# The 64-row products of a two-block kernel alternate between two PSUM banks and the two row halves, and the second feed-forward takes its spare weight buffers later

## The chip, the cores and the metric

The kernel runs on one core of one Trainium2 chip. The metric is device microseconds of one execution, the median of three runs. The engines are named as the profile names them: PE (TensorE, the matrix engine), DVE (VectorE), ACT (ScalarE), POOL (GpSimd) and SP (SyncE, which issues the loads).

## The reference, cut to what matters

256 rows of 1024 numbers pass through a two-layer block and then a hybrid block, all in fp32. The parts that the change touches:

```python
# layer 1: gated linear attention, 4 heads, chunks of 64 rows
state = state * dec[..., None] + jnp.einsum('bhtk,bhtv->bhkv', ke, vv)
...
# layer 2: chunk attention, 16 heads of 64
s = jnp.einsum('bhtd,bhjd->bhtj', qi, kb).astype(jnp.float32) + bias
p = jax.nn.softmax(jnp.where(mb, s, NEG_INF), axis=-1).astype(vb.dtype)
return jnp.einsum('bhtj,bhjd->bhtd', p, vb)
...
# after each of the two layers: y = squared_relu_mlp(u, w1, w2), then a layer norm
...
# hybrid block: 8 index heads of 64 choose the 64 best keys, 8 heads of 64 attend to them
s = jnp.einsum('bqhd,bkd->bhqk', iqb, ik).astype(jnp.float32) * (IDX_DIM ** -0.5)
score = jnp.einsum('bqh,bhqk->bqk', w, jax.nn.relu(s))
_, idx = lax.top_k(score, k_top)
sc = jnp.einsum('bqhd,bqkhd->bhqk', qb, kg).astype(jnp.float32) * (Dh ** -0.5)
p = jax.nn.softmax(sc, axis=-1)
```

The contraction of the state update is over 64 rows of a chunk, that of the scores and index scores over the 64 numbers of a head. These are the 64-row products of the title. Every other matrix product contracts over 128 partitions at a time.

## The kernel before, in words

The 256 rows are two halves of 128, h = 0 and h = 1. The program passes through six phases: gated linear attention, feed-forward, chunk attention, second feed-forward, hybrid mixer, convolutional feed-forward. In each, weights arrive in chunks of 128x1024 fp32 that SP loads into one of four buffers `raw`. ACT rounds a chunk to a high part (`hi`, line 257) and DVE takes the difference as a low part (`lo`, line 262); a product is then three matmuls, `mm3` (lines 266 to 268). There are eight pairs of `hi` and `lo`. A few chunks, named by a table (`_spare`, lines 172 to 180), take another pair instead, `qk0`/`v0` or `qk1`/`v1`: the buffers in which the attentions keep keys and values. In the second feed-forward these are its second chunk and every fifth after it.

The kernel's PSUM tiles are banks of 128x512 fp32: two for tag `pc`, two for `ps` (projections), four for `y`. The score loop `core_scores` (lines 742 to 765) takes one `y` bank at a time. A bank holds 512 score columns: four heads of 128 keys for h = 0, two heads of 256 keys for h = 1. `banks` orders the heads so that one bank holds only even heads, whose queries and keys lie in partitions 0 to 63, and the next only odd heads, in partitions 64 to 127. The bank's matmuls (line 754) are followed by an addition on DVE (line 817 in chunk attention, 934 in the hybrid mixer), the maximum on DVE (758), one exponential a head on ACT (760), and, after the next bank's scores have been written down, four transposes on PE (373, operands `const` and `cs`) and a copy on ACT (769). The products with the values (line 780) come later. The loop is a generator: each `next` is called between chunks of the value projection, so that matmuls of that projection stand between the banks.

The chunk attention does its heads in two groups of eight, g = 0 and 1, each for both halves. The index scores (line 908) fill two banks (h = 0) or four (h = 1), one after another. The states of gated linear attention (line 727) use partitions 0 to 63 for the first chunk of a half and 64 to 127 for the second.

The order on each engine is not written by hand: a list scheduler orders the instructions from their dependences, estimated costs and priorities, and `prefetch` decides when a weight load may be issued. So an edit in one place moves instructions around it on every engine. Between scores DVE also works through products of the conditioning vector with its weights (line 300), one 128x1024 pass for each loaded block.

Of the kernel before, what the change touches and what calls it, by code (L numbers as in the profile page):

```python
# [172 lines left out]
def _spare():  # L173

    out = {}
    for a, b, pairs in ((ENDS[0] - 1, ENDS[1] + 1, (0, 1)), (ENDS[2] - 4, ENDS[2] - 3, (0,)),
                        (ENDS[2] + 1, ENDS[3] + 1, (0, 1)), (ENDS[4] - 8, ENDS[5], (0, 1))):
        for n, i in enumerate(range(a, b, SP)):
            out[i] = pairs[n % len(pairs)]
    return out  # L180
# [5 lines left out]
class K:  # L186
# [450 lines left out]
    def gla_core(self, h, lr, q, k, v, box):  # L637
# [57 lines left out]
        S2 = self.states(h, 0, er, v, dec)  # L695
# [9 lines left out]
        if h == 0:  # L705
            self.S = S2
            self.S = self.states(h, 1, er, v, dec)
# [10 lines left out]
    def states(self, h, c, er, v, dec):  # L718

        nc = self.nc  # L720
        out = []
        r = slice(c * 64, c * 64 + 64)
        for j in range(2):
            p = self.pc()
            for d2 in range(2):
                d = j * 2 + d2
                nc.tensor.matmul(p[:, d2 * 256:d2 * 256 + 256], er[r, d * 128:d * 128 + 128], v[r, d * 256:d * 256 + 256], start=True, stop=True)
            S = self.sb(512, "bias", 4)
            if self.S is None:
                nc.scalar.activation(S, p, AF.Copy)  # L730
            else:
                for d2 in range(2):
                    hs = slice(d2 * 256, d2 * 256 + 256)
                    nc.vector.scalar_tensor_tensor(S[:, hs], self.S[j][:, hs], dec[:, j * 2 + d2, c:c + 1], p[:, hs], op0=ALU.mult, op1=ALU.add)
            out.append(S)
        return out
# [5 lines left out]
    def core_scores(self, h, qT, kT, pts, sums, score):  # L742
# [5 lines left out]
        last = None  # L748

        for n, hs in enumerate(self.banks(nb)):  # L750
            p = self.bank()
            for i, hd in enumerate(hs):
                r0 = (hd % 2) * 64
                nc.tensor.matmul(p[:, i * N:i * N + N], qT[r0:r0 + 64, hd // 2, :], kT[r0:r0 + 64, hd // 2, :N], start=True, stop=True)  # L754
            s = score(hs[0], nb, p)
            sv = s.rearrange("p (a n) -> p a n", n=N)
            mx = self.sb(4, "mx", 4)
            nc.vector.tensor_reduce(mx[:, :nb], sv, axis=AX.X, op=ALU.max, negate=True)
            for i in range(nb):
                nc.scalar.activation(sv[:, i, :], sv[:, i, :], AF.Exp, bias=mx[:, i:i + 1], accum_out=sums[:, hs[i]:hs[i] + 1])  # L760
            if last is not None:
                self.core_turn(last, pts[n - 1])
            last = s
            yield
        self.core_turn(last, pts[n])
# [105 lines left out]
    def hyb_phase(self, h, after):  # L871
# [32 lines left out]
        for hs in self.banks(nb):  # L904
            p = self.bank()
            for i, hd in enumerate(hs):
                r0 = (hd % 2) * 64
                nc.tensor.matmul(p[:, i * N:i * N + N], iqT[r0:r0 + 64, hd // 2, :], self.ikT[r0:r0 + 64, :N], start=True, stop=True)
            rl = self.cs()[:, :512]
            nc.scalar.activation(rl, p, AF.Relu, scale=0.125)  # L910
            for i, hd in enumerate(hs):
                if hd == 0:
                    nc.vector.tensor_scalar(sc, rl[:, 0:N], iw[:, 0:1], None, op0=ALU.mult)
                else:
                    nc.vector.scalar_tensor_tensor(sc, rl[:, i * N:i * N + N], iw[:, hd:hd + 1], sc, op0=ALU.mult, op1=ALU.add)
# [21 lines left out]
        qT = None  # L937
# [455 lines left out]
```

## Time and profile before

| | |
|---|---|
| three runs | 1060.17, 1054.99, 1059.1 us; median 1059.1 us |
| the profiled execution | 1057.73 us, of which its span is 1055.9 us |
| busy share of the span | PE 96%, DVE 72%, ACT 54%, POOL 3% |
| mean granted TensorE clock | 0.995 |
| DMA | 228.98 MB, mean 217 GB/s |

The span runs from the first to the last recorded instruction; 1.8 us of the execution lie outside it. "Busy" on PE counts a matmul from its start to a modelled end, and matmuls overlap in that count, so the pitch from one start to the next is what a matmul costs. The trace shows each fp32 matmul of the 64-row products as two instructions. An engine's row in a timeline begins with its start and its length in us, and ends in brackets with the idle time before it and the instruction that ended that idle time.

### The profile page before, as it was taken

The numbers are of one execution on the slowest core, as the hardware profiler recorded it, in microseconds if no ns is written. First come the engines' busy times: TensorE is split into PE (matmuls) and PEld (weight loads), VectorE is DVE, ScalarE is ACT, GpSimd is POOL, SyncE is SP. The second block draws the span as 40 slices with busy tenths as digits, with TensorE's granted clock in tenths as the row PEclk, the third lists the DMA queues.
The fourth block names the chain that finished last, engine by engine and source line by source line (L and its number), as shares of the span: only waits on it lengthen the run. The fifth ranks groups of instructions, "written<-read, shape, count | busy, mean of one in ns | idle before, by whom it ended". The sixth has DMA issues, their size and how long they took to land.

```text
span 1055.9 us, 15168 instructions
## 1 busy us (share of the span) xinstructions
PE 1017.6 (96%) x5628; PEld 850.0 (80%) x5628; DVE 763.3 (72%) x1186; ACT 567.6 (54%) x869; POOL 33.8 (3%) x77
## 2 busy tenths in 40 slices
PE   6999999999998999999999999999999999999997
PEld 4777777898986758677889988777878788999996
DVE  6878898777677886749656644898445678877764
ACT  4664466545455454536655553576454378555543
POOL 0000200000000000000000000000000001000000
PEclk9999999999999999999999999999999999999999
DMA  9888868888885787825877654344346455655521
GB/s 341 331 298 301 309 201 282 306 304 298 284 297 179 218 295 247 286 92 184 287 229 249 227 166 145 120 145 149 106 164 213 162 179 182 217 185 192 183 80 40
DMA packets 69478, 228.98 MB, mean 217 GB/s; under 512 B 7430, under 2 KB 12806, under 8 KB 69404
## 3 DMA queue, kind: packets, MB, share of 16 engines
q1 hardware_dynamic: 69404, 228.01, 64.2%
q8 instruction: 44, 0.72, 0.3%
q14 instruction: 30, 0.25, 0.1%
HBM read 226.93 MB, written 1.05 MB: 216 GB/s over the span
## 4 chain that ended last, share of the span: by engine, by line
PE 63%; DVE 9%; DMA 7%; ACT 3%; issue 3%; POOL 1%; POOLq 0%; DVEq 0%; ACTq 0%; SPq 0%
PE ps L268 12%; PE ps L266 12%; PE ps L267 12%; PE y L266 8%; PE y L268 8%; PE y L267 7%; DMA raw<-in_w_dram 6%; DVE lo L262 2%; PE y L780 1%; PE pc L373 1%; ACT hi L257 1%; DMA raw<-in_ada_dram 1%; PE y L373 1%; PE y L754 1%; DVE x L393 1%
## 5 line engine op out<-in xcount | busy, mean ns | idle before, releaser
L262 DVE TENSOR_TENSOR lo<-raw,hi 128x1024 fp32r<-128x1024 f32 (+3 forms) x290 | 306.5, 1068 | 132.8 <-ACT hi L257 129.4
L257 ACT ACTIVATE hi<-raw 128x1024 fp32r<-128x1024 f32 (+2 forms) x250 | 262.4, 1054 | 252.1 <-PE y L268 66.9
L266 PE MATMUL ps<-hi,uh 128*128 128x512 f32 (+3 forms) x408 | 160.4, 394 | 2.3 <-ACT uh L365 0.9
L267 PE MATMUL ps<-lo,uh 128*128 128x512 f32 (+3 forms) x408 | 158.2, 388 | 1.2 <-DVE lo L1260 1.1
L266 PE MATMUL y<-hi,hh 128*128 128x512 f32 x378 | 152.9, 404 | 5.3 <-ACT hh L274 5.2
L268 PE MATMUL ps<-hi,ul 128*128 128x512 f32 (+3 forms) x408 | 157.5, 386 | 0.2 <-DVE ul L366 0.2
L267 PE MATMUL ps<-ul,hi 128*128 128x256 f32 x536 | 151.4, 282 | 0.0
L268 PE MATMUL ps<-uh,lo 128*128 128x256 f32 x536 | 151.1, 282 | 0.0
L266 PE MATMUL ps<-uh,hi 128*128 128x256 f32 x536 | 151.0, 282 | 0.0
L268 PE MATMUL y<-hi,hl 128*128 128x512 f32 x378 | 149.8, 398 | 0.4 <-DVE hl L275 0.4
L267 PE MATMUL y<-lo,hh 128*128 128x512 f32 x378 | 150.2, 397 | 0.0
L266 PEld LDWEIGHTS ps<-uh,hi 128*128 128x128 f32 x536 | 100.9, 188 | 2.3
L267 PEld LDWEIGHTS ps<-ul,hi 128*128 128x128 f32 x536 | 100.6, 188 | 2.3
L268 PEld LDWEIGHTS ps<-uh,lo 128*128 128x128 f32 x536 | 101.3, 189 | 0.0
L266 PEld LDWEIGHTS ps<-hi,uh 128*128 128x128 f32 x408 | 77.5, 190 | 19.3 <-ACT uh L365 1.5
L267 PEld LDWEIGHTS ps<-lo,uh 128*128 128x128 f32 x408 | 77.5, 190 | 16.8 <-DVE lo L1260 3.0
L268 PEld LDWEIGHTS ps<-hi,ul 128*128 128x128 f32 x408 | 77.4, 190 | 15.8 <-issue 0.9
L266 PEld LDWEIGHTS y<-hi,hh 128*128 128x128 f32 x378 | 71.5, 189 | 21.4 <-ACT hh L274 6.6
L268 PEld LDWEIGHTS y<-hi,hl 128*128 128x128 f32 x378 | 71.3, 189 | 18.2 <-DVE hl L275 1.2
L267 PEld LDWEIGHTS y<-lo,hh 128*128 128x128 f32 x378 | 71.4, 189 | 14.8 <-issue 0.7
L262 DVE TENSOR_TENSOR v<-raw,qk 128x1024 fp32r<-128x1024 f32 (+1 forms) x49 | 52.0, 1069 | 26.7 <-ACT qk L257 26.1
L257 ACT ACTIVATE qk<-raw 128x1024 fp32r<-128x1024 f32 x42 | 44.5, 1060 | 49.7 <-DMA raw<-in_w_dram 28.7
(290 smaller groups left out, 1500.0 us busy)
## 6 DMA issues: line engine op xcount, KB each, us to landing
raw<-in_w_dram SPq DMA_DIRECT2D x302, 512.0 KB, 4.3
raw<-in_ada_dram SPq DMA_DIRECT2D x80, 512.0 KB, 4.6
br<-in_rows_dram SPq DMA_DIRECT2D x12, 256.0 KB, 5.4
bias<-in_relb_dram SPq DMA_DIRECT2D x12, 256.0 KB, 6.2
lng<-in_rows_dram SPq DMA_DIRECT2D x5, 512.0 KB, 4.8
raw<-in_w_dram SPq DMA_DIRECT2D x8, 256.0 KB, 6.7
lnb<-in_rows_dram SPq DMA_DIRECT2D x4, 512.0 KB, 6.1
z<-in_ada_dram SPq DMA_DIRECT2D x3, 512.0 KB, 7.4
```

What stands on the lines that cost most here:

```text
L257: self.nc.scalar.activation(hi, raw, AF.Copy)
L262: self.nc.vector.tensor_sub(lo[:, sl], raw[:, sl], hi[:, sl].bitcast(F32))
L266: mm(out, xh, wh, start=start, stop=False)
L267: mm(out, xh, wl, start=False, stop=False)
L268: mm(out, xl, wh, start=False, stop=stop)
L373: self.nc.tensor.transpose(p[:, k * 128:k * 128 + 128], src[:, k * 128:k * 128 + 128], self.ident)
L393: nc.vector.tensor_mul(x[:, sl], x[:, sl], self.lng[:, sl])
L754: nc.tensor.matmul(p[:, i * N:i * N + N], qT[r0:r0 + 64, hd // 2, :], kT[r0:r0 + 64, hd // 2, :N], start=True, stop=True)
L780: nc.tensor.matmul(o[:, hd * 64:hd * 64 + 64], pT[:, (i * nkb + kb) * 128:(i * nkb + kb) * 128 + 128], v[:, kb, hd * 64:hd * 64 + 64], sta ...
```

## The change

Three places are rewritten and one number is moved. `states` makes the products of both chunks of a half together where both are wanted (h = 0), with one `pc` bank for each chunk, and alternates between the chunks. `core_scores` takes two `y` banks at a time, one of even and one of odd heads, and alternates between them matmul by matmul; only then come the additions, maxima and exponentials of both banks, and after them the transposes of the two banks before. It yields twice for each two banks. The index scores alternate in the same way. In `_spare` the first chunk of the second feed-forward that takes a spare pair is its sixth where it was its second.

```diff
-                        (ENDS[2] + 1, ENDS[3] + 1, (0, 1)), (ENDS[4] - 8, ENDS[5], (0, 1))):
+                        (ENDS[2] + 5, ENDS[3] + 1, (0, 1)), (ENDS[4] - 8, ENDS[5], (0, 1))):
...
-        S2 = self.states(h, 0, er, v, dec)
+        S2, *S3 = self.states(er, v, dec, 2 - h)
...
+            ps = [self.pc() for _ in range(n)]
             for d2 in range(2):
                 d = j * 2 + d2
-                nc.tensor.matmul(p[:, d2 * 256:d2 * 256 + 256], er[r, d * 128:d * 128 + 128], v[r, d * 256:d * 256 + 256], start=True, stop=True)
...
+                for c, p in enumerate(ps):
+                    r = slice(c * 64, c * 64 + 64)
+                    nc.tensor.matmul(p[:, d2 * 256:d2 * 256 + 256], er[r, d * 128:d * 128 + 128], v[r, d * 256:d * 256 + 256], start=True, stop=True)
...
-        for n, hs in enumerate(self.banks(nb)):
-            p = self.bank()
-            for i, hd in enumerate(hs):
-                r0 = (hd % 2) * 64
-                nc.tensor.matmul(p[:, i * N:i * N + N], qT[r0:r0 + 64, hd // 2, :], kT[r0:r0 + 64, hd // 2, :N], start=True, stop=True)
...
+        for n in range(0, len(groups), 2):
+            two = groups[n:n + 2]
+            ps = [self.bank() for _ in two]
+            for hs in zip(*two):
+                for p, hd in zip(ps, hs):
+                    i = two[hd % 2].index(hd)
+                    r0 = (hd % 2) * 64
+                    nc.tensor.matmul(p[:, i * N:i * N + N], qT[r0:r0 + 64, hd // 2, :], kT[r0:r0 + 64, hd // 2, :N], start=True, stop=True)
+            new = []
+            for hs, p in zip(two, ps):
+                s = score(hs[0], nb, p)
...
+                new.append(s)
+            for m, s in enumerate(last):
+                self.core_turn(s, pts[n - 2 + m])
+            last = new
             yield
-        self.core_turn(last, pts[n])
+            yield
+        for m, s in enumerate(last):
+            self.core_turn(s, pts[n + m])
```

The work is the same, and so is the number of matmuls of each kind but for the spare chunks (12 in the second feed-forward, before 13). The 64-row products stood in 26 unbroken runs on PE and stand in 19. In the changed file the scores are at line 761, the maximum at 767, the copy at 781 and the index scores at 922.

First, PE in the first head group of the chunk attention, where h = 0's second score bank and h = 1's first were apart. Before, from h = 0's first bank (`y_3478`; `y_3506` is h = 1's first, `y_3530` h = 0's second):

```order
L754 MATMUL y_3478<-qk_668_3243,ep_677_3285 128x128 x2
L266 MATMUL ps_3499<-hi_3256,uh_72 128x512
L267 MATMUL ps_3499<-lo_3257,uh_72 128x512
L268 MATMUL ps_3499<-hi_3256,ul_73 128x512
L266 MATMUL ps_3499<-hi_3256,uh_72 128x512
L267 MATMUL ps_3499<-lo_3257,uh_72 128x512
L268 MATMUL ps_3499<-hi_3256,ul_73 128x512
L754 MATMUL y_3506<-qk_668_3243,ep_692_3368 128x256 x2
```

After, the same place (`y_3478` and `y_3479` are h = 0's two banks), from the second of two pieces into which its scores are split:

```order
L761 MATMUL y_3478<-qk_668_3243,ep_677_3285 128x128
L761 MATMUL y_3479<-qk_668_3243,ep_677_3285 128x128
L761 MATMUL y_3478<-qk_668_3243,ep_677_3285 128x128
L761 MATMUL y_3479<-qk_668_3243,ep_677_3285 128x128
L761 MATMUL y_3478<-qk_668_3243,ep_677_3285 128x128
L761 MATMUL y_3479<-qk_668_3243,ep_677_3285 128x128
L266 MATMUL ps_3515<-hi_3256,uh_72 128x512
L267 MATMUL ps_3515<-lo_3257,uh_72 128x512
L268 MATMUL ps_3515<-hi_3256,ul_73 128x512
```

Both banks of h = 0 now stand together and alternate. Behind them come three more `mm3`-matmuls, h = 1's two banks, and then 18 matmuls of the projection before the first transposes of `cs`.

Second, PE in the second head group, at the first transposes. Before, the transposes of h = 0's first bank (`cs_3948`) stand seven rows behind h = 1's first scores:

```order
L754 MATMUL y_3968<-qk_777_3673,ep_805_3805 128x256 x2
L266 MATMUL ps_3933<-hi_3731,uh_72 128x512
L267 MATMUL ps_3933<-lo_3732,uh_72 128x512
L268 MATMUL ps_3933<-hi_3731,ul_73 128x512
L266 MATMUL ps_3933<-hi_3731,uh_72 128x512
L267 MATMUL ps_3933<-lo_3732,uh_72 128x512
L268 MATMUL ps_3933<-hi_3731,ul_73 128x512
L754 MATMUL y_3992<-qk_777_3673,ep_802_3786 128x128 x4
L373 MATMUL y_4008<-const_70,cs_3948 128x128 x4
```

After, the last rows of the 18 projection matmuls that follow h = 1's scores, and the transposes of both of h = 0's banks (`cs_3953`, `cs_3964`):

```order
L266 MATMUL ps_3933<-hi_3769,uh_72 128x512
L267 MATMUL ps_3933<-lo_3770,uh_72 128x512
L268 MATMUL ps_3933<-hi_3769,ul_73 128x512
L373 MATMUL y_4042<-const_70,cs_3953 128x128 x4
L373 MATMUL y_4048<-const_70,cs_3964 128x128 x4
L266 MATMUL ps_3977<-hi_3769,uh_72 128x512
L267 MATMUL ps_3977<-lo_3770,uh_72 128x512
```

Eight transposes now stand together, behind three times as many projection matmuls.

Third, DVE at the start of the second feed-forward. Before, the low part of its second chunk (`v_922`, of the spare pair) stands behind the residual and the statistics of h = 1 (`x_10`):

```order
L405 SCALAR_TENSOR_TENSOR x_10_75<-x_10_75,z_4394 128x512
L366 TENSOR_TENSOR ul_73<-t_911_4261,uh_72 128x512
L406 BN_STATS st_4395<-x_10_75 128x6
L262 TENSOR_TENSOR v_922_4337<-raw_4334,qk_921_4336 128x512
L408 BN_AGGR mv_4402<-st_4395 128x2
L262 TENSOR_TENSOR v_922_4337<-raw_4334,qk_921_4336 128x512
```

After, the second, third and fourth chunk (`lo_4288`, `lo_4305`, `lo_4322`, all of the eight ordinary pairs) stand among the norm of h = 0 (`x_9`), ahead of h = 1's residual:

```order
L262 TENSOR_TENSOR lo_4288<-raw_4285,hi_4287 128x512
L410 TENSOR_SCALAR rv_4238<-mv_4236 128x1
L262 TENSOR_TENSOR lo_4288<-raw_4285,hi_4287 128x512
L412 TENSOR_SCALAR rv_4238<-mv_4236,rv_4238 128x1
L275 TENSOR_TENSOR hl_928_4346<-y_4340,hh_927_4345 128x512
L414 TENSOR_SCALAR x_9_74<-x_9_74,rv_4238 128x512
L262 TENSOR_TENSOR lo_4305<-raw_4302,hi_4304 128x512 x2
L262 TENSOR_TENSOR lo_4322<-raw_4319,hi_4321 128x512
L393 TENSOR_TENSOR x_9_74<-x_9_74,lng_3233 128x512
L262 TENSOR_TENSOR lo_4322<-raw_4319,hi_4321 128x512
```

The second chunk's low part moved up some 20 rows on DVE, and the third's and fourth's with it.

## Rows read from the trace of the kernel before

**Rows 1.** The page, busy time: engine, us, share of the span, instructions.
```profile
PE 1017.6 (96%) x5628; PEld 850.0 (80%) x5628; DVE 763.3 (72%) x1186; ACT 567.6 (54%) x869; POOL 33.8 (3%) x77
```
**Rows 2.** What PE waited for: us in total, times, longest us.
```profile
PE y L373 <- ACT cs L760: 2.9, 4, 1.3
PE ps L267 <- DVE v L262: 2.3, 1, 2.3
```
**Rows 3.** PE's timeline at a states run: start us, length us.
```profile
97.31 1.99 PE L727 MATMUL pc<-v,hl 64*128 64x256 f32 x8 [1.01 <-DVE z L693]
99.23 0.70 PE L704 MATMUL y<-bias,cs 128*128 128x256 f32 x2
```
**Rows 4.** PE's timeline around two score runs of the first head group.
```profile
375.20 0.40 PE L268 MATMUL ps<-hi,ul 128*128 128x512 f32 x1
375.53 1.13 PE L754 MATMUL y<-qk,ep 64*128 64x256 f32 x4
376.58 0.50 PE L266 MATMUL ps<-hi,uh 128*128 128x512 f32 x1
376.92 0.40 PE L267 MATMUL ps<-lo,uh 128*128 128x512 f32 x1
377.15 0.40 PE L268 MATMUL ps<-hi,ul 128*128 128x512 f32 x1
...
378.18 1.16 PE L754 MATMUL y<-qk,ep 64*128 64x128 f32 x8
379.27 0.51 PE L266 MATMUL ps<-hi,uh 128*128 128x512 f32 x1
```
**Rows 5.** PE's timeline at the index scores and one hybrid score run.
```profile
690.90 1.71 PE L908 MATMUL y<-ikT,t 64*128 64x128 f32 x16
692.54 0.42 PE L266 MATMUL ps<-hi,uh 128*128 128x328 f32 x1
...
701.76 2.10 PE L908 MATMUL y<-ikT,t 64*128 64x256 f32 x16
703.79 0.50 PE L268 MATMUL ps<-hi,ul 128*128 128x512 f32 x1
...
727.32 1.17 PE L754 MATMUL y<-qk,ep 64*128 64x256 f32 x12
728.66 0.33 PE L373 MATMUL y<-const,cs 128*128 128x128 f32 x1 [0.17 <-ACT cs L760]
```
**Rows 6.** PE's timeline, three transposes that waited.
```profile
390.28 0.33 PE L373 MATMUL y<-const,cs 128*128 128x128 f32 x1 [1.31 <-ACT cs L760]
...
441.29 0.33 PE L373 MATMUL y<-const,cs 128*128 128x128 f32 x1 [1.07 <-ACT cs L760]
...
712.92 0.66 PE L373 MATMUL pc<-const,t 128*128 128x128 f32 x4 [1.83 <-DVE t L869]
```
**Rows 7.** DVE's timeline in the first head group.
```profile
378.79 1.22 DVE L300 SCALAR_TENSOR_TENSOR raw<-raw,crow 128x1024 f32<-128x1024 f32 x1
...
383.10 0.68 DVE L758 TENSOR_REDUCE mx<-cs 128x2 f32<-128x512 f32 x1
```
**Rows 8.** ACT's timeline, the first and last exponential of one bank of four heads.
```profile
378.91 0.40 ACT L760 ACTIVATE cs<-cs,mx 128x128 f32<-128x128 f32 x1 [3.52 <-DVE mx L758]
...
380.37 0.19 ACT L760 ACTIVATION_READ_ACCUMULATOR cs<-cs,mx 128x1 f32 x1
```
**Rows 9.** PE's timeline at the start of the second feed-forward.
```profile
482.45 0.39 PE L266 MATMUL ps<-hi,uh 128*128 128x512 f32 x1
485.16 0.50 PE L267 MATMUL ps<-v,uh 128*128 128x512 f32 x1 [2.31 <-DVE v L262]
```
**Rows 10.** Stretches: us, busy time of each engine, PEclk, DMA share, GB/s.
```profile
486.00:489.30 3.30, 3.30 (x10) 2.47 (x10) 2.86 (x7) 0.81 (x1) 0.84 (x1) 0.53 0.64 210
713.00:720.00 7.00, 7.00 (x34) 5.62 (x35) 7.00 (x19) 3.97 (x5) 0.00 (x0) 1.00 0.39 130
```
**Rows 11.** DVE's timeline in the hybrid mixer, a step of the top-k search.
```profile
712.86 0.40 DVE L921 MATCH_REPLACE8 gnorm<-m,gnorm 128x256 f32<-128x256 f32 x1
```

More of the change, by code (lines that the diff above doesn't have):

```diff
@@ L705, in gla_core @@
         if h == 0:
-            self.S = S2
-            self.S = self.states(h, 1, er, v, dec)
+            self.S = S3[0]
         yield
@@ L716, in gla_core, with states @@
         box["r"] = r
-    def states(self, h, c, er, v, dec):
+    def states(self, er, v, dec, n):
         nc = self.nc
-        out = []
-        r = slice(c * 64, c * 64 + 64)
+        out = [[], []]
         for j in range(2):
-            p = self.pc()
+            ps = [self.pc() for _ in range(n)]
             for d2 in range(2):
                 d = j * 2 + d2
-                nc.tensor.matmul(p[:, d2 * 256:d2 * 256 + 256], er[r, d * 128:d * 128 + 128], v[r, d * 256:d * 256 + 256], start=True, stop=True)
[L728 to L736, printed above, removed]
+                for c, p in enumerate(ps):
+                    r = slice(c * 64, c * 64 + 64)
+                    nc.tensor.matmul(p[:, d2 * 256:d2 * 256 + 256], er[r, d * 128:d * 128 + 128], v[r, d * 256:d * 256 + 256], start=True, stop=True)
+            for c, p in enumerate(ps):
+                S = self.sb(512, "bias", 4)
+                before = out[0][j] if c else self.S and self.S[j]
+                if before is None:
+                    nc.scalar.activation(S, p, AF.Copy)
+                else:
+                    for d2 in range(2):
+                        hs = slice(d2 * 256, d2 * 256 + 256)
+                        nc.vector.scalar_tensor_tensor(S[:, hs], before[:, hs], dec[:, j * 2 + d2, c:c + 1], p[:, hs], op0=ALU.mult, op1=ALU.add)
+                out[c].append(S)
+        return out[:n]
     @staticmethod
@@ L747, in core_scores @@
         nb = 512 // N
-        last = None
-        for n, hs in enumerate(self.banks(nb)):
-            p = self.bank()
-            for i, hd in enumerate(hs):
-                r0 = (hd % 2) * 64
-                nc.tensor.matmul(p[:, i * N:i * N + N], qT[r0:r0 + 64, hd // 2, :], kT[r0:r0 + 64, hd // 2, :N], start=True, stop=True)
[L755 to L763, printed above, removed]
+        groups = self.banks(nb)
+        last = []
+        for n in range(0, len(groups), 2):
[9 more added lines that the diff above has]
+                s = score(hs[0], nb, p)
+                sv = s.rearrange("p (a n) -> p a n", n=N)
+                mx = self.sb(4, "mx", 4)
+                nc.vector.tensor_reduce(mx[:, :nb], sv, axis=AX.X, op=ALU.max, negate=True)
+                for i in range(nb):
+                    nc.scalar.activation(sv[:, i, :], sv[:, i, :], AF.Exp, bias=mx[:, i:i + 1], accum_out=sums[:, hs[i]:hs[i] + 1])
+                new.append(s)
+            for m, s in enumerate(last):
+                self.core_turn(s, pts[n - 2 + m])
+            last = new
             yield
-        self.core_turn(last, pts[n])
+            yield
+        for m, s in enumerate(last):
+            self.core_turn(s, pts[n + m])
     def core_turn(self, s, pT):
@@ L903, in hyb_phase @@
         sc = self.scam[:, h * 256:h * 256 + N]
[L904 to L915, printed above, removed]
+        groups = self.banks(nb)
+        for two in (groups[n:n + 2] for n in range(0, len(groups), 2)):
+            ps = [self.bank() for _ in two]
+            for i, hs in enumerate(zip(*two)):
+                for p, hd in zip(ps, hs):
+                    r0 = (hd % 2) * 64
+                    nc.tensor.matmul(p[:, i * N:i * N + N], iqT[r0:r0 + 64, hd // 2, :], self.ikT[r0:r0 + 64, :N], start=True, stop=True)
+            for hs, p in zip(two, ps):
+                rl = self.cs()[:, :512]
+                nc.scalar.activation(rl, p, AF.Relu, scale=0.125)
+                for i, hd in enumerate(hs):
+                    if hd == 0:
+                        nc.vector.tensor_scalar(sc, rl[:, 0:N], iw[:, 0:1], None, op0=ALU.mult)
+                    else:
+                        nc.vector.scalar_tensor_tensor(sc, rl[:, i * N:i * N + N], iw[:, hd:hd + 1], sc, op0=ALU.mult, op1=ALU.add)
         nc.gpsimd.affine_select(sc, sc, pattern=[[-1, N]], base=h * 128, channel_multiplier=1, compare_op=ALU.is_ge, fill=NEG)
```

## The prediction

> **What bounds the kernel now.** I read the page first, then PE's waits, then PE's timeline in the stages that the change touches. On the page PE is busy for 96% of the span and no other engine comes near [rows 1]; the reader is to see that time is won where PE issues less or waits less, and hardly elsewhere. PE's waits are few. Those of the touched stages are four for exponentials (2.9 us), one for a low part of a weight chunk (2.3 us) [rows 2], and one for the rotation of a query or key (1.8 us) [rows 6]. The rest of the touched stages is PE issuing matmuls back to back, so I price those from start to start.
>
> **Price of a 64-row run.** Eight 256-column instructions of the states take 99.23 - 97.31 = 1.92 us [rows 3], four of the scores 376.58 - 375.53 = 1.05 us [rows 4]. The difference gives 0.217 us for one and 0.18 us fixed. Eight of 128 columns take 379.27 - 378.18 = 1.09 us [rows 4], less 0.18 that is 0.114 each. At the run's edges the pitch of the neighbours grows from 0.23 to 0.33 and 0.34 us [rows 4], 0.21 more. An unbroken run thus costs 0.39 us beside its instructions.
>
> **Price of two row halves at once.** The kernel before shows this already, by accident of order, where banks of opposite halves stand next to each other. Sixteen 256-column index instructions would take 16 x 0.217 + 0.18 = 3.65 us one by one; they took 2.03 [rows 5], so 1.62 of a possible 1.74 was hidden (93%). They change halves every four instructions. The run of four 256-column and eight 128-column instructions would take 1.96; it took 1.34 - 0.17 = 1.17 [rows 5], 0.79 of 0.87 hidden. The index run that changes halves only once, after eight instructions, took 1.64 instead of 2.00 [rows 5]: 0.36 of 0.91. So halves overlap when they are in different banks and within a few instructions of each other. The new order alternates every matmul, that is every two instructions, which no row shows. I take the 93%; the bounds are 40%, from the run that changes once, and 100%.
>
> The Trainium skill, page "TensorEngine Tiling (Array Packing)", section "Key Properties", says that different tiles of the array can load weights and multiply in parallel, with no reserve. By that rule all would be hidden, and the sum below would be 0.6 us larger; the rows show 93% at best [rows 5], and I go by them.
>
> **The change part by part.** Runs are counted in the order of the engine, before and after.
> - Chunk attention, first head group: 10 runs become 6, 4 x 0.39 = 1.56 us. Hidden: eight 128-column instructions (0.91), four 256-column (0.87), and of the last four only two (0.43), because transposes stand between the others; 2.21 x 0.93 = 2.05. Together 3.6.
> - Second group: 6 runs become 3, 1.17. Hidden 0.91 + 0.87 + 0.87 = 2.65, x 0.93 = 2.46. Together 3.6.
> - Hybrid scores: 5 runs become 4, 0.39. Hidden 0.68 + 0.87 + 0.87 = 2.42 (one pair is cut by transposes), x 0.93 = 2.25, less the 0.79 that was hidden before. Together 1.85.
> - Index scores: h = 0 gets 0.91 x 0.93 - 0.36 = 0.5; h = 1 overlapped already, 0.
> - States: 3 runs become 4, -0.39; two chunks now stand side by side and could hide 0.87. But two `pc` banks are all there are, and the third bank waits for a copy of the first. I take 0, with -0.4 and +0.5 as bounds.
>
> PE's issue falls by 9.55 us. Against it stand the waits, since the second bank of a pair now ends its softmax behind the first. An addition and a maximum take about 0.6 us each (their length of 0.68 less its overlap) [rows 7], a bank's exponentials 380.37 + 0.19 - 378.91 = 1.65 [rows 8].
> - First group: DVE alternates these steps with conditioning passes of 1.2 us [rows 7], and the order puts the second bank's maximum into the place of the one at 383.10. It ends at 383.7, and the first transpose of that bank can start near 384.3, a head after. PE's rows up to there (6 matmuls, a pair run, 18 matmuls, four transposes, 5 matmuls) end near 383.0: a wait of 1.3 us. For the next pair I find another 0.7. The old wait of 1.31 [rows 6] goes. Net -0.7, bounds 0 and -2.3.
> - Second group: from the end of h = 0's scores to the transposes PE has 6 + 18 matmuls at 0.234 and a pair run, 6.9 us. The second bank needs 0.6 x 3 for addition, addition and first maximum, then 2 x 1.65 on ACT, 5.1 us. It is covered by 1.8 us, and the old wait of 1.07 [rows 6] disappears: +1.1. If that cover were gone the price is the same 1.3 as in the first group.
> - Hybrid mixer: the rotation that PE waited for (1.83 us) [rows 6] comes two search steps later, about 0.4 us each [rows 11], but four more matmuls (0.94 us) stand ahead of its transpose: 0. The next rotation but one stands behind one more 128x1024 pass (1.2 us, as the conditioning pass) [rows 7]: -1.0. Behind h = 1's first scores PE has only 3 + 9 matmuls and a few edges, 4.0 us, where the second bank needs 5.1: -1.1; after the last pair -0.6. Net -2.7, bounds 0 and -4.5.
>
> The same page's section "Performance Considerations", under "PSUM Bottleneck", speaks against the change: tiling makes TensorE faster, not the emptying of PSUM, which can become the limit. The lengths of the steps that empty the banks bear it out so far [rows 7, 8]; the first rival below is this mechanism, and by the rule the result would be its 1054.7 us.
>
> **The spare chunks.** PE stood for 2.31 us before the low part of the second chunk [rows 9], because DVE made it behind the residual and statistics of h = 1. Behind that wait PE's granted clock was 0.53 for 3.30 us [rows 10], 0.47 x 3.30 = 1.55 us of work lost; the wait of 1.83 us that ended at 712.92 left the clock at 1.00 [rows 6, 10]. In the new order the low parts of chunks two to four stand on DVE ahead of h = 1's residual, the second's some 20 rows earlier. The wait and its half clock, 3.9 us, should go. DVE then does about one half-pass more (0.6 us) before the inputs of h = 0, whose readers have some slack; I take off 0.6. Net +3.2, bounds 0 (the wait only moves to another chunk or to h = 1's norm) and +3.9. What is late next is h = 1's norm, with 22 matmuls of cover behind its place.
>
> **Sum.** 9.55 - 0.7 + 1.1 - 2.7 + 3.2 = 10.4 us off. The profiled execution took 1057.7 us, 1.8 of it outside the span, and would take 1047.3; against the median of the three runs, 1059.1, it is 1048.7. I say 1048.5. The three runs themselves lie 0.5% apart, and about 0.5% (5.3 us) is what this measurement can tell from no change.
>
> **The rivals.**
> - *The softmax eats it.* The second bank's exponentials wait behind the first's, and the projection's matmuls don't cover them. I counted 3.7 us of such waits at three places; if each of the six score pairs costs its full 1.65 us [rows 8], that is 9.9, 6.2 more: 1054.7 us. For: DVE and ACT already end PE's waits here [rows 2]. Against: 18 matmuls stand behind two of the pairs. Chance 0.17.
> - *The halves don't overlap in the new pattern.* Every change of half costs like a run's edge, so that alternating each matmul hides nothing. Then only the fewer runs remain, 3.1 us, and the 2.8 us hidden before are lost; with the waits and the spare chunks as above the gain is 0.3 - 0.7 + 1.1 - 2.7 + 3.2 = 1.2: 1057.9. Against it speak three rows [rows 5]. Chance 0.08.
> - *The ordinary pairs run short.* Chunks two to five of the second feed-forward all need one of the eight ordinary pairs while the attention's output weights still hold some, loads are held back, and the 3.2 us turn into a loss of the same size: 1054.9. For: the chunk in the spare pair needed none of the eight. Against: it was just this chunk that came late. Chance 0.07.
> - *Slower.* A pair takes two of the four `y` banks and its transposes two more, so a late copy holds up both. If PE stands at a pair for 0.6 + 0.6 + 1.65 = 2.85 us, that is longer than the 2.31 after which the clock fell, and the half clock adds 1.55: 4.4 us a place. Without the counted waits the gain is 14.1, so it is used up at three to four of the six places and the kernel is slower by over 0.5% from five; at all six, 1071. Against: it needs the same long wait where 6.9 us of matmuls stand over a need of 5.1. Chance 0.06.
>
> My forecast has the remaining 0.62. Without any new wait, with the whole 3.9 and the states at +0.5 it reaches 1044; with only 40% hidden (8.2 x 0.53 = 4.3 less) and no gain from the spare chunks, 1056. The range is 1043.5 to 1057, which holds most of the first and third rival too. Faster by over 0.5% means below 1053.8: all but a little of the forecast and a part of two rivals, 0.68; within 0.5% 0.26; slower 0.06.
>
> **What would show it.** Right: pair runs of four 256-column matmuls (eight instructions) in about 1.1 us instead of 1.9, of eight 128-column matmuls (16 instructions) in about 1.1 instead of 2.0; no wait for a low part and a clock of 1.00 at the start of the second feed-forward; PE's sum of waits for exponentials near 4 us. Wrong: runs that take the serial time (no overlap); waits of 1.5 us and more before transposes in every group (softmax); waits for `raw`, `hi` or `lo` in the second feed-forward (pairs short); stretches with a clock near 0.5 in the attention (slower).

## The result: 0.5% faster, a little over half of what was forecast

| | before | after |
|---|---|---|
| median, 20 runs each on one chip | 1057.96 us | 1052.11 us |
| range of the runs | 1052.91 to 1064.66 | 1047.91 to 1059.25 |
| profiled execution, span | 1057.73, 1055.9 us | 1050.37, 1048.6 us |
| mean granted clock | 0.995 | 0.991 |

The ratio is 0.995, with a 95% interval from 0.9931 to 0.997: 5.9 us between the medians, where the forecast was 10.6 (1048.5 against 1059.1). The interval leaves no doubt of the sign; it doesn't tell 4 us from 7.

The pairs of banks run as they were meant to. PE's timeline after, at a pair run of the first head group and at the first run of index scores:

```profile
373.68 1.13 PE L761 MATMUL y<-qk,ep 64*128 64x256 f32 x8
374.74 0.50 PE L266 MATMUL ps<-hi,uh 128*128 128x512 f32 x1
...
684.04 1.16 PE L922 MATMUL y<-ikT,t 64*128 64x128 f32 x16
685.13 0.42 PE L266 MATMUL ps<-hi,uh 128*128 128x328 f32 x1
```

Eight 256-column instructions take 374.74 - 373.68 = 1.06 us. Four took 1.05 before [rows 4] and eight of the states 1.92 [rows 3]. Sixteen of 128 columns take 1.09 us, as eight did [rows 4]. In these runs the second half of the work costs nothing. The start of the second feed-forward is also as forecast: PE no longer waits for a low part of a weight chunk there [rows 9].

What PE waited for after (us in total, times, longest), the rows that answer to [rows 2] and the new ones:

```profile
PE pc L373 <- DVE t L851: 2.5, 2, 1.8
...
PE pc L373 <- DVE t L881: 2.4, 3, 1.9
PE y L792 <- DVE v L846: 1.8, 1, 1.8
PE y L373 <- ACT cs L769: 1.6, 2, 0.8
```

The wait for the low part (`v L262`, 2.3 us) is gone and those for exponentials look smaller. A new one has come: the value products (line 792) wait 1.8 us for DVE's addition to the values (line 846). PE's timeline in the second head group shows more than the list does:

```profile
432.33 3.02 PE L373 MATMUL y<-const,cs 128*128 128x128 f32 x8 [0.79 <-ACT cs L769]
435.11 0.48 PE L266 MATMUL ps<-hi,uh 128*128 128x512 f32 x1
...
437.76 1.09 PE L373 MATMUL y<-const,cs 128*128 128x128 f32 x8
438.60 0.48 PE L266 MATMUL ps<-hi,uh 128*128 128x512 f32 x1
...
443.21 1.79 PE L792 MATMUL y<-v,gnorm 128*128 128x64 f32 x8 [1.78 <-DVE v L846]
444.76 0.77 PE L266 MATMUL ps<-hi,hh 128*128 128x512 f32 x1
445.33 0.63 PE L267 MATMUL ps<-lo,hh 128*128 128x512 f32 x1
```

The first eight transposes take 2.78 us, the next eight 0.84: between the first ones PE waits head by head, another 1.9 us inside one row. And behind the 1.78 us the matmuls of 512 columns last 0.63 instead of 0.39 us. The stretches from there on (length, busy time by engine, PEclk, DMA share, GB/s):

```profile
443.20:446.50 3.30, 3.29 (x14) 3.00 (x14) 2.30 (x4) 0.93 (x4) 0.00 (x0) 0.53 0.76 206
446.50:449.00 2.50, 2.50 (x10) 2.31 (x11) 0.98 (x2) 0.00 (x0) 0.00 (x0) 0.50 0.85 324
449.00:453.00 4.00, 4.00 (x18) 2.93 (x18) 2.41 (x7) 1.66 (x2) 0.00 (x0) 0.84 0.51 147
```

The clock is at the lower of its two levels, 1.2 instead of 2.4 GHz, for some 7 us: 0.47 x 3.3 + 0.50 x 2.5 + 0.16 x 4 = 3.4 us of work lost. In the first group the waits for the key transposes (1.81 at 368.75) and for exponentials are about as long as before.

Where the time went is read best by counting. The products of weights (lines 266 to 268) are 4824 in both traces, in nearly one order, so the start of the n-th tells how far ahead a kernel is. The table gives the gain over the profiled execution of before between such marks, for every kernel below too: the first head group (before: 361.4 to 427.0 us), the second (to 457.5), the start of the second feed-forward (478.0 to 513.6), and the hybrid mixer (660.1 to 769.8).

| kernel | group 1 | group 2 | 2nd FF start | hybrid | whole | ratio to before, 95% interval |
|---|---|---|---|---|---|---|
| changed | +2.2 | -2.0 | +3.2 | +1.2 | +7.4 | 0.995 (0.9931 to 0.997) |
| spare_only | -1.2 | +0.7 | +2.7 | +1.0 | -0.1 | 0.9971 (0.9945 to 0.9997) |
| no_spare | +2.8 | -1.8 | +0.5 | +0.7 | +2.3 | 0.9998 (0.9973 to 1.0023) |
| one_half | +2.8 | +2.1 | +3.1 | 0.0 | +8.6 | 0.9942 (0.9915 to 0.9968) |
| bank_by_bank | -3.4 | +0.8 | +2.8 | +2.1 | +1.9 | 0.9935 (0.9907 to 0.9963) |
| spread | -1.5 | +2.5 | +2.7 | +1.6 | +3.3 | 0.998 (0.9955 to 1.0004) |
| hi_first | +3.2 | +0.3 | +2.8 | +0.4 | +8.4 | 0.9946 (0.9918 to 0.9973) |
| g1_single | -1.2 | -0.2 | +2.9 | +1.2 | +2.5 | 0.9957 (0.9928 to 0.9985) |
| bias_no_load | +0.9 | +1.9 | +2.7 | +1.5 | +2.8 | 0.9963 (0.9932 to 0.9994) |
| att_one_half | +2.3 | +1.2 | +2.9 | +1.2 | +10.2 | 0.9933 (0.9911 to 0.9955) |
| att_single | +2.0 | +0.7 | +2.6 | +1.5 | +5.7 | 0.9972 (0.9953 to 0.9991) |
| ada_no_load | +6.6 | +4.4 | +2.2 | +1.5 | +21.8 | 0.9807 (0.9782 to 0.9832) |
| warm | +0.7 | +0.2 | +2.5 | +1.6 | +4.2 | 0.9969 (0.9952 to 0.9986) |

A row is one execution. Waits and the clock behind them differ from one execution to the next: spare_only has the attention of before, and its first group came out 1.2 us longer. Before the attention too, a wait at the end of the first feed-forward, which the change doesn't touch, and the half clock beside it cost up to 3.7 us more than in before. The column of the second feed-forward hardly moves among the kernels with the new spare table; those of the attention are to be read as a tendency. The ratio is made from 4 runs of a kernel (ada_no_load) to 20, against runs of before on the same chip. The profiled executions of spare_only and bank_by_bank were the slowest of theirs, 5.8 and 7.5 us above their medians.

### The profile page after: what moved, and what is told of

It is laid out like the page before. It is cut to its first block, busy times and chain, and to the rows that moved or that the text cites. A ratio compares the mean times of both kernels' runs of the same rounds, so it can differ in the third digit from the quotient of the medians.

```text
span 1048.6 us, 15164 instructions
## 1 busy us (share of the span) xinstructions
PE 1011.4 (96%) x5628; PEld 845.8 (81%) x5628; DVE 760.1 (72%) x1186; ACT 567.0 (54%) x869; POOL 35.4 (3%) x77
## 3 DMA queue, kind: packets, MB, share of 16 engines
HBM read 226.93 MB, written 1.05 MB: 217 GB/s over the span
## 4 chain that ended last, share of the span: by engine, by line
PE 50%; DMA 13%; DVE 11%; issue 6%; ACT 5%; POOL 1%; POOLq 0%; ACTq 0%; SPq 0%; DVEq 0%
DMA raw<-in_w_dram 12%; PE ps L266 9%; PE ps L268 9%; PE ps L267 9%; PE y L266 6%; PE y L268 6%; PE y L267 6%; DVE lo L262 4%; ACT hi L257 3%; PE y L792 2%; PE pc L373 1%; DVE raw L300 1%; DMA bias<-in_relb_dram 1%; PE y L373 1%; ACT cs L769 1%
## 5 line engine op out<-in xcount | busy, mean ns | idle before, releaser
L262 DVE TENSOR_TENSOR lo<-raw,hi 128x1024 fp32r<-128x1024 f32 (+3 forms) x293 | 307.5, 1062 | 128.4 <-ACT hi L257 122.5
L262 DVE TENSOR_TENSOR v<-raw,qk 128x1024 fp32r<-128x1024 f32 (+1 forms) x46 | 50.7, 1106 | 27.3 <-ACT qk L257 27.0
```

What stands on the lines that cost most here:

```text
L262: self.nc.vector.tensor_sub(lo[:, sl], raw[:, sl], hi[:, sl].bitcast(F32))
```

## The experiments

Theory F: the attention is not bound by PE's issue but by a chain of weight load, ACT and DVE, so what PE saves there becomes waiting, partly at half clock. The theory of the prediction: PE's issue bounds it, with waits of known size on top. Theory A says that each half of the change gives what the prediction gave it; G, that loads alone set the pace; B to E are stated where they come up.

### Each half alone

```diff
 spare_only = before, with
-                        (ENDS[2] + 1, ENDS[3] + 1, (0, 1)), (ENDS[4] - 8, ENDS[5], (0, 1))):
+                        (ENDS[2] + 5, ENDS[3] + 1, (0, 1)), (ENDS[4] - 8, ENDS[5], (0, 1))):
 no_spare = the changed kernel without that line
```

spare_only: 

> The kernel before with the new spare table alone. Theory A (the second feed-forward gains by itself): the wait of 2.31 us for the second chunk's low part and the half clock behind it go, about 3.2 us of the 7.3 us by which the profiled execution became shorter; ratio to before about 0.997, gain against the same matmul of before unchanged up to the output projection of the attention, then +3.2. Theory B (the spare chunks only help because the attention before them ends otherwise): no gain, ratio 1.000, and a wait for a low part remains.

no_spare: 

> The changed kernel with the old spare table. Theory A: the pairs of banks keep what they gave in the changed kernel up to the end of the attention (2.7 us at the start of the second feed-forward, of which about 1.3 are start-up), the 2.3 us wait and the half clock at the start of the second feed-forward are back, and the hybrid mixer gives 1.2 us; ratio about 0.998. Theory C (the attention's second group loses by the way in which the new spare table orders the weight loads ahead): the loss of 2.0 us in the second head group disappears, ratio about 0.996.

Spare chunks alone: 0.9971. Pairs alone: 0.9998, within 0.3% of nothing either way. PE's timeline of no_spare at the start of the second feed-forward has the old wait back:

```profile
481.45 0.39 PE L266 MATMUL ps<-hi,uh 128*128 128x512 f32 x1
484.16 0.51 PE L267 MATMUL ps<-v,uh 128*128 128x512 f32 x1 [2.31 <-DVE v L262]
```

Its clock stayed at 1.00 from 484 to 488 us in this execution, where before lost 1.55 us behind the same wait at 0.53 [rows 10]. That it stands at only +0.5 is due in part to a wait of 0.62 us at 504.53 that before didn't have. Theories B and C fall: the new table gains with the old attention before it, and without it the second group still loses 1.8 us. The 0.9 us that spare_only gains at the start of the hybrid mixer belong to the new table as well, since no_spare lacks them.

### The halves apart

```diff
 one_half: scores and index scores; att_one_half: the attention's scores alone
-                    r0 = (hd % 2) * 64
+                    r0 = 0
```

one_half: 

> The changed kernel with every score and index score taken from partitions 0 to 63 (odd heads then repeat the even heads' scores: the output is not the reference's). Order, banks and sizes stay. Theory A (two row halves at once are what makes a pair run short): runs of eight 256-column instructions take 1.9 us and not 1.06, runs of sixteen 128-column instructions 2.0 and not 1.09; PE's issue grows by about 9 us, of which waits in the attention swallow some: 4 to 9 us longer than the changed kernel, 1056 to 1061 us. Theory D (only fewer and longer runs count): run lengths and the time stay, 1052 us.

att_one_half: 

> The changed kernel with the attention's scores taken from partitions 0 to 63 for every head (odd heads repeat the even heads' scores: the output is not the reference's); index scores and hybrid scores alternate halves as in the changed kernel. Order, banks and sizes stay; PE's issue in the attention grows by about 5 us. Theory F (what PE saves in the attention becomes waiting there, and waiting costs the clock): no longer than the changed kernel, ratio to before 0.991 to 0.996, clock near 1.00 in the attention. The theory of the prediction (PE's issue bounds the attention): 5 us longer than the changed kernel, ratio about 1.000.

The runs answer as theory A says. PE's timeline of one_half, a pair run of the second group and what follows:

```profile
437.43 1.99 PE L761 MATMUL y<-qk,ep 64*128 64x256 f32 x8
439.35 1.09 PE L373 MATMUL y<-const,cs 128*128 128x128 f32 x8
...
443.96 1.10 PE L792 MATMUL y<-v,gnorm 128*128 128x64 f32 x8 [0.95 <-DVE v L846]
444.87 0.48 PE L266 MATMUL ps<-hi,hh 128*128 128x512 f32 x1
```

Eight instructions take 1.92 us: theory D falls, two row halves are what made 1.06 of it. But the kernel with the longer runs is not slower, where theory A had 4 to 9 us. Both ratios, 0.9942 and 0.9933, lie at or below that of the changed kernel, with overlapping intervals. The value products wait 0.95 us instead of 1.78, and no half clock follows. The whole attention, from the mark at its start to the last, is one row for each kernel; that of att_one_half, then that of the changed kernel, then that of before (columns as above):

```profile
359.16:451.70 92.54, 89.51 (x451) 69.00 (x450) 71.14 (x109) 50.20 (x108) 1.80 (x8) 1.00 0.86 282
```
```profile
358.89:454.82 95.93, 89.09 (x450) 67.31 (x449) 71.20 (x109) 50.30 (x108) 1.80 (x8) 0.96 0.83 274
```
```profile
361.36:457.47 96.11, 91.41 (x449) 68.26 (x448) 70.71 (x106) 49.27 (x104) 1.80 (x8) 1.00 0.81 273
```

PE has about 5 us more to issue in att_one_half and its attention is 3.4 us shorter. The prediction's theory, 5 us longer than the changed kernel, would be a ratio of 0.9998; the interval of att_one_half ends at 0.9955. The theory falls.

A good part of what PE saves goes into the clock, and not in the profiled executions alone. The mean granted clock was taken in every run. It is 0.9911 on average over the 32 runs of the changed kernel and no_spare, 0.9932 over the 93 runs of before beside the experiments, and 0.9947 over the 16 runs of one_half and att_one_half. Over 1050 us the kernels whose pairs alternate between the halves thus lose 2.2 us more work to the clock than before and 3.8 us more than those of one half.

```diff
 bank_by_bank: the scores of two banks, one bank after the other
-            for hs in zip(*two):
-                for p, hd in zip(ps, hs):
-                    i = two[hd % 2].index(hd)
+            for p, hs in zip(ps, two):
+                for i, hd in enumerate(hs):
```

> The changed kernel with two banks at a time in the scores, but one bank's matmuls before the other's; index scores and states as changed. Theory A (halves overlap when they are a few instructions apart): h = 1's pairs, which then change halves after four instructions, still take about 1.1 us; h = 0's, which change after eight, take about 1.64 instead of 1.09, so the kernel is about 1.5 us longer than the changed one. Theory E (only matmul by matmul alternation overlaps): all pairs take the serial time, 7 us more of PE issue.

PE's timeline of bank_by_bank, a pair of each size:

```profile
431.78 1.71 PE L760 MATMUL y<-qk,ep 64*128 64x128 f32 x16
433.42 0.50 PE L266 MATMUL ps<-hi,uh 128*128 128x512 f32 x1
...
435.02 1.14 PE L760 MATMUL y<-qk,ep 64*128 64x256 f32 x8
436.09 0.50 PE L266 MATMUL ps<-hi,uh 128*128 128x512 f32 x1
```

1.64 us is to the digit what [rows 5] gave for a change of half after eight instructions; 1.07 for a change after four fits the 2.03 us there for twice as many. So for h = 1 alternating matmul by matmul wins nothing over bank by bank, for h = 0 it wins 0.55 us a pair. Theory E falls. By its ratio the time is that of the changed kernel, where theory A had it 1.5 us longer; the intervals overlap too far to tell.

### Softmax, rounding and old loop

```diff
 spread: the second bank's softmax one projection chunk later
                 new.append(s)
+                if len(new) == 1:
+                    yield
...
             last = new
-            yield
             yield
...
 hi_first: in the attention's weights
+            with self.tc.high_priority(offset=HPE):
+                self.nc.scalar.activation(hi, raw, AF.Copy)
...
 g1_single: the loop of before, as core_single, in group g = 1; att_single: in both groups
+                    core = (self.core_single if g else self.core_scores)(h, qT, kT, pts, sums, score)
```

spread: 

> The changed kernel, but the second bank of a pair gets its addition, maximum and exponentials one projection chunk later (a yield between the two banks' softmax instead of two behind them). The pairs' matmuls stay as they are. Theory F (the attention is bound by the chain from weight load over ACT's exponentials and DVE's low parts to the value addition, and what PE saves turns into waits there, two of them with a half clock): with the exponentials apart, the low parts on DVE don't stand for 3.5 us behind them, the wait of 1.78 us for the value addition falls under 1 us and the half clock behind it goes: second head group 3 to 5 us better, 1047 to 1049 us. Theory G (bunching has nothing to do with it; the loads alone set the pace): within 1.5 us of the changed kernel.

hi_first: 

> The changed kernel with the rounding of a weight chunk on ACT at a higher priority in the attention's weights; in the order this moves one of them ahead of the last two of the twelve exponentials in the second head group, and others by a few places. Theory F: DVE's idle stretch of 3.5 us before the low part becomes about 2.4, the value addition comes about 1 us sooner, PE's wait for it falls to about 0.8 and the half clock goes: 3 us better, about 1049. Theory G: within 1.5 us of the changed kernel.

g1_single: 

> The changed kernel with the old loop, one bank at a time, for the second head group of the attention alone. Theory F: the second group's loss of 2.0 us goes, for its PE time was never the bound there; 1 to 3 us better than the changed kernel, 1049 to 1051. The theory of the prediction (the pairs are worth 3.6 us of PE time there and the loss is from elsewhere): 3 us or more longer than the changed kernel, 1055.

att_single: 

> The changed kernel with the old loop, one bank at a time, in both head groups of the attention; hybrid mixer, index scores, states and spare chunks as changed. Theory F: the pairs are worth little in the attention, so within 2 us of the changed kernel, ratio to before 0.995 to 0.998 from the spare chunks (2.8 us) and the hybrid mixer (1.2 us). The theory of the prediction: without the pairs' 7 us, ratio 0.999 or more, once the spare chunks and the hybrid mixer are counted 1053 us or more.

None of the four can be told from the changed kernel. spread came out at 0.998, where theory F had it 3 to 5 us better. Its profile got its 4.5 us in the second group and lost 3.7 in the first, where its clock fell; the mean clock of its twelve runs, 0.988, is the lowest of all kernels. This speaks against bunched exponentials as the cause of the waiting, without excluding that they add to it. hi_first gained 2.3 us in the second group, less than the 3 forecast, and the ratio is the same. g1_single, 1 to 3 us better by theory F, came out at 0.9957, no better: inconclusive. att_single at 0.9972 is 2.3 us longer than the changed kernel by the ratios, where theory F had 2 at most, with intervals that overlap: whatever the pairs give in the attention, it is not the 7 us of PE time.

### Loads

```diff
 bias_no_load: no load of the position bias
-                nc.sync.dma_start(out=bias, in_=bass.AP(tensor=R.tensor, offset=R.offset + (g * 8 + h0) * 384 + 1, ap=[[1, 128], [768, nh], [1, N]]))
+                nc.gpsimd.memset(bias, 0.0)
 ada_no_load: no load of conditioning weights for the second layer
-                nc.sync.dma_start(out=raw, in_=src(k))
+                if layer == 0:
+                    nc.sync.dma_start(out=raw, in_=src(k))
+                else:
+                    nc.vector.tensor_copy(raw[:, 0:1], self.crow[:, 0:1])
...
-                    nc.vector.scalar_tensor_tensor(raw, raw, 1.0, self.crow,
+                    nc.vector.scalar_tensor_tensor(raw, raw if layer == 0 else self.crow, 1.0, self.crow,
```

bias_no_load: 

> The changed kernel without the twelve loads of the position bias (the bias is zero, so the attention lacks it). Theory G (DMA sets the pace of the attention): weight chunks land sooner, the load that took 8.9 us from issue to landing in the second group takes under 7, and the attention gains 3 us and more: 1048 or less. Theory F (ACT's and DVE's chain sets it): under 1.5 us.

ada_no_load: 

> The changed kernel without the second layer's loads of the conditioning weights (DVE's passes run on a row that is there already, so the modulation of the second layer is not the reference's); the weight chunks then have the load queue and the four raw buffers nearly for themselves in the attention. Theory G (the weight stream sets the pace of the attention): waits for exponentials, for the value addition and the key transposes in the attention fall from about 7 us to under 3 and the clock stays near 1.00: 5 us or more better than the changed kernel, ratio under 0.990. Theory F in its narrow form (only ACT's and DVE's bunched softmax): within 2 us of the changed kernel.

Without the bias nothing changes that could be told, where theory G had 3 us. Without the conditioning loads the kernel is 20 us shorter than before: +6.2 at the end of the first feed-forward, where a wait of 4.4 us and its half clock go, and +10.9 in the attention (96.11 us before, 85.18 here). The same stretch of the attention in ada_no_load, and its wait for the value addition, from the views of stretches and of PE's waits:

```profile
354.86:440.04 85.18, 83.98 (x458) 65.58 (x456) 71.83 (x124) 49.72 (x110) 1.81 (x8) 1.00 0.64 208
```
```profile
PE y L795 <- DVE v L849: 0.6, 1, 0.6
```

DVE and ACT are as busy there as before (71.8 and 49.7 us) and PE is hardly idle: 1.2 us against 6.8 in the changed kernel and 4.7 in before. DMA moves 208 GB/s instead of 274. So the attention waits on its loads, together with what stands behind them in order. Theory F in its narrow form, softmax alone, falls with it. The chain that ended last, of the changed kernel in the second group (start, us, what), shows the path:

```profile
421.81 8.92 DMA raw<-in_w_dram
...
430.83 1.06 ACT hi L257
431.89 3.09 ACT cs L769 x16
...
435.02 0.33 PE y L373
...
437.82 1.04 PE y L373 x8
...
439.49 0.68 DVE lo L262
440.17 1.20 DVE cs L829 x2
...
441.88 0.67 DVE mx L767
442.55 0.61 DVE v L846
...
443.21 1.79 PE y L792 x8
```

A weight chunk lands 8.9 us after its issue; ACT stands before its rounding until 430.83, and the exponentials of four banks stand behind it in order. They run to 436.8; two copies and the next chunk's rounding follow. ACT's and DVE's timelines have the start of it:

```profile
425.87 1.06 ACT L257 ACTIVATE qk<-raw 128x1024 fp32r<-128x1024 f32 x1 [3.02 <-DMA raw<-in_w_dram]
430.83 1.06 ACT L257 ACTIVATE hi<-raw 128x1024 fp32r<-128x1024 f32 x1 [3.90 <-DMA raw<-in_w_dram]
```
```profile
426.96 1.22 DVE L262 TENSOR_TENSOR v<-raw,qk 128x1024 fp32r<-128x1024 f32 x1 [3.30 <-ACT qk L257]
```

ACT twice stands for a chunk that has not landed. DVE stands 3.30 us behind the first of them, so the additions to h = 0's scores, whose run on PE ends at 424.40, begin only at 428.10. DVE's timeline has the other end:

```profile
438.88 1.29 DVE L262 TENSOR_TENSOR lo<-raw,hi 128x512 fp32r<-128x512 f32 x2 [3.47 <-PE y L373]
440.09 1.28 DVE L829 TENSOR_TENSOR cs<-y,bias 128x512 f32<-128x512 f32 x2
441.29 1.26 DVE L767 TENSOR_REDUCE mx<-cs 128x2 f32<-128x512 f32 x2
442.47 0.68 DVE L846 TENSOR_TENSOR v<-ps,br 128x512 f32<-128x512 f32 x1
```

DVE stands for 3.47 us before that chunk's low part (the wait is put down to PE's transposes, whose copies stood ahead of the rounding on ACT), and behind it in order come two additions, two maxima and only then the value addition for which PE waits. What ada_no_load doesn't settle is how much of the 10.9 us is the load queue itself and how much DVE, whose conditioning passes also no longer wait for data with softmax steps behind them: the kernel takes both away at once.

### PE time that costs nothing

```diff
 warm: ahead of the first transposes of a score pair in the attention
+            self.nc.tensor.matmul(p, mx[:, 0:1].to_broadcast([128, 128]), self.cst[:, :512], start=True, stop=True)
```

> The changed kernel with a matmul of no use (512 columns, fp32, about 0.87 us) ahead of the first transposes of each score pair of the attention, into the bank that the transposes then overwrite; it waits for the maximum of the bank whose exponentials are awaited. Six in all, about 5 us of PE work added. Theory F: PE has that time to spare and the clock falls less often: within 1.5 us of the changed kernel or better, and less clock lost in the attention than the 3.3 us of the changed kernel's profile. The theory of the prediction: 5 us longer, ratio about 1.000.

The added matmuls show in PE's timeline, and the attention's stretch (columns as above) keeps its clock:

```profile
436.30 1.02 PE L373 MATMUL y<-const,mx 128*128 128x512 f32 x2
```
```profile
362.27:457.53 95.26, 88.47 (x461) 66.34 (x460) 71.30 (x108) 49.60 (x108) 1.80 (x8) 1.00 0.82 274
```

Some 5 us of useless PE work left the attention at 95.3 us, against 95.9. The ratio, 0.9969, is 2.0 us above the changed kernel's (theory F had 1.5 at most), with intervals that overlap, and not 5 us, which would be 0.9998: by these ratios more than half of the added work found room, but it wins nothing that can be measured. The mean clock of the twelve runs is 0.9938, against 0.9910 in the changed kernel. The wait for the value addition stays; it is longer in this execution, and the clock behind it was 1.00 from 448 to 452 us:

```profile
PE y L794 <- DVE v L848: 3.0, 1, 3.0
```

Apart from ada_no_load, which leaves loads out, none of the versions beats the changed kernel by more than its interval.

## Why the prediction held, and which term failed

**Held: the price of a run and of two halves.** Runs forecast at about 1.1 us take 1.06 and 1.09, and one_half puts the serial price at 1.92 and 1.98. The hidden share is not 93% but all of it. The Trainium skill's page "TensorEngine Tiling (Array Packing)", section "Key Properties", by which different tiles of the array work in parallel, was nearer, and 1.06 against 1.92 us agree with it; the 0.6 us more that the prediction worked out from it can't be told in the time. The states stayed serial, as taken: twelve instructions in 2.88 us. The new code alternates between their chunks, but the order that ran does not: one bank follows the other, and within a bank each instruction starts 0.22 to 0.32 us after the last, where alternating scores start 6 to 7 ns apart in twos.

**Held: the spare chunks.** +3.2 us forecast, +3.2 in the profile, +2.2 to +3.1 in the eleven other kernels with the new table, and 0.9971 alone: 0.29% of the measured 0.50%.

**Held in size, not in parts: the hybrid mixer.** Pairs and index scores were put at 2.35 us of issue less 2.7 of waits, -0.35. The profile has +1.2, but +0.9 of it is the spare table's; what the pairs leave is about 0.2 to 0.3. Beside spare_only, which has the same table, PE is busy 1.6 us less there and idle 1.4 us more: both terms were too large.

**Failed: the attention.** The prediction gave it 3.6 - 0.7 in the first group and 3.6 + 1.1 in the second, 7.6 us. The profile has +2.2 and -2.0, and the pairs alone measure 0.9998. The issue was saved: ada_no_load, where PE hardly waits, gains 10.9 there, 3.5 of it as waits that before had too (4.7 less 1.2), so 7.4 is left for the forecast's 7.2. The step that failed is the one on the second group: "It is covered by 1.8 us". I counted DVE's 1.8 us of additions and maxima and ACT's 3.3 us of exponentials from the scores, as if both were free. DVE began 3.7 us after the scores, and ACT stood at a rounding for a chunk still on its way until 430.83, so the transposes waited 0.8 and 1.9 us. And nowhere did I ask for the value addition, queued on DVE behind the next chunk's low part: 1.8 us, and 3.4 at half clock. Together 7.9 us of new loss stand against 3.6 saved and the old waits gone; I had counted none of it. The old waits were more than the 1.07 us that I took. PE's timeline before:

```profile
437.89 0.93 PE L373 MATMUL y<-const,cs 128*128 128x128 f32 x4 [0.30 <-ACT cs L760]
438.58 0.48 PE L266 MATMUL ps<-hi,uh 128*128 128x512 f32 x1
...
441.29 1.10 PE L373 MATMUL y<-const,cs 128*128 128x128 f32 x3 [1.07 <-ACT cs L760]
442.15 0.48 PE L266 MATMUL ps<-hi,uh 128*128 128x512 f32 x1
```

Another 0.30 us stands ahead of one bank, and four and three transposes there take 0.69 and 0.86 us, about 0.8 us more than at the pace of the 0.84 us that eight take when they don't wait. With 2.2 us of old waits the sum is 3.6 + 2.2 - 7.9 = -2.1, and -2.0 was measured. The 3.4 us at half clock are this execution's; over all runs the pairs lose 2.2 us to the clock against before.

**The rivals.** "The softmax eats it" named the symptom and a result of 1054.7, nearer to 1052.1 than my 1048.5, but not the cause: in the chain the exponentials come late because a load does, and without the conditioning loads the waits are gone. The Trainium skill's page "TensorEngine Tiling (Array Packing)", section "Performance Considerations", under "PSUM Bottleneck", says that copying out of PSUM may become the limit after a fourfold speedup. That would have put the limit at the copies; no run here shows it there. The half clock that I kept for the slower case came after 1.8 us at one place already. "The halves don't overlap" and "the ordinary pairs run short" are refuted, by the runs and by the clean start of the second feed-forward.

The number, 1048.5, is 3.6 us under the median. Two accidents of sampling lie on the way: the median of before is 1.1 us lower with 20 runs than with three, and the profiled execution of the changed kernel lies 1.7 us under its median. That the number lies no further off is in part luck. The attention was to give 7.6 of the 10.4 us and gave 0.2 in the profile; 2.5 of the profile's 7.4 us were gained ahead of the attention, where the change touches the states alone, for which nothing was forecast, and where spare_only, with the code of before, lost 3.6.

## What to carry to other kernels

A share of 96% busy PE doesn't say that each stage is bound by PE. Ask of the stage: if PE needed nothing, what would its time be? In this attention the loads, the rounding and the softmax in order behind them held the stage at 91 to 99 us in the profiles of all kernels with their conditioning loads, in no order of PE's work; an experiment that makes PE slower there, or takes loads away, tells this. When work is bunched on PE, follow every engine's queue one step further than the instruction that PE waits for, to what stands behind a load.

## What the hardware showed unexpectedly

Saved matmuls can cost a good part of their time in clock: 5 us more issue in the attention (one_half and att_one_half) came with 3.8 us less lost to the clock. Behind a wait of 1.78 us in the second group the clock stood at 0.53 and 0.50 for nearly 6 us; a wait of 1.83 us in before [rows 6, 10], 2.31 us in no_spare and 3.0 us in warm left it at 1.00, and 2.31 us in before [rows 9, 10] did not. So the length of the last wait doesn't decide by itself. In the group that lost its clock PE had already stood still between transposes 8 us earlier. More than that the runs don't show.
